# Extra weight sums of the down projection: the kept block copied from DRAM to DRAM, all sums in two bursts, and three fixed rooms for reading them back

## The chip, the cores and the metric

The kernel runs on one core of a Trainium2 chip. The metric is the device time of one execution in microseconds (us); the time of a kernel is the median of its runs. The core has a matrix engine (TensorE, in the profile PE, with its weight loads as PEld), a vector engine (VectorE, DVE), a scalar engine (ScalarE, ACT), a general engine (GpSimd, POOL) and a sync engine that here only issues DMAs (SyncE, SP). Sixteen DMA engines move data; SP's DMAs go through the queue that the profile calls q1, POOL's through q0, ACT's through q10. Engines run their instructions in order and wait for each other by semaphores.

## What is computed

One decoder layer on 256 tokens with 2048 features, all in float32. Two token mixers work in parallel on the same normalised input, a gated recurrence and a sliding-window attention with sinks; gates merge them; a squared-ReLU MLP of width 8192 follows. Cut to the lines that matter:

```python
h = rmsnorm(x, norm_mix_pre)
xr, yr, q, k, v, g_rnn, g_attn = split(h @ w_in)
y_rnn = rg_lru(conv(xr)) * gelu(yr)
y_att = attention(rope(q), rope(k), v, sinks)
mix = sigmoid(g_rnn) * (y_rnn @ w_rnn_proj) + sigmoid(g_attn) * (y_att @ w_attn_proj)
x = x + rmsnorm(mix @ w_out, norm_mix_post)
h = rmsnorm(x, norm_mlp_pre)
u = square(relu(h @ w_mlp_up))          # 2048 -> 8192
x = x + rmsnorm(u @ w_mlp_down, norm_mlp_post)   # 8192 -> 2048
```

## The kernel before

**Matrix products in three parts.** Every float32 operand is split in two, a high half in a format that PE takes at full rate and a low half that holds the rest. A product is three matmuls: high by high, high by low, low by high. The weights come through `Stream` (the object `ws`): chunks of 128 x 2048 are loaded in halves of 512 KB on SP (L87, into `wraw` or, late in the kernel, `xraw`), ACT rounds a half to `whi` (L109), DVE subtracts it to `wlo` (L110), PE multiplies. `load_to` and `split_to` run a few halves ahead of PE; `begin` is called at each step of the stream and steps the side jobs in `ws.side`.

**Order of the stages.** First `kx`: sixteen tiles that hold a piece of the key and value weights and of the transposed input, loaded on SP (L425) and used by the `kv` matmuls (L496). Then the gate weights and the input itself (`xq`, L433, for the norm's sums of squares, L502). Then four attention groups, each eight weight halves for a gate `g` and eight for `q`, with the rope of `q` on DVE (L592 to L596: `ra`, `rb`, `qr`) and PE's transposes of it (`pq`, L637) among the matmuls; then the recurrence, the merge of both mixers (gate by projection on DVE, L953 and L954, PE's transposes `ptr`, L936), the output projection, and the MLP in two halves, f = 0 and f = 1. Each half of the MLP has 16 up products of pairs (`up_pair`, `a_pair`) and two down passes (`down`, n = 0 and n = 1) over 16 weight chunks each.

**The down passes with fewer products.** For most down chunks PE forms seven block products in place of eight. This needs extra sums of the chunk's quarters (128 x 512 each): T1, T2, T3 and T4. A table (`KINDS`) says for each chunk how many of these are made ahead: all four (kind 4), two (kind 2) or none (kind 3); kind 1 is a plain chunk. There are 36 chunks of kinds 2 and 4, 18 in each half of the MLP.

**`sums_ahead(c)`** makes them for one chunk long before the down pass. It is a generator and each `yield` is one step of the weight stream. It loads the chunk (1 MB) on POOL into a room `early` (L370), waits four steps, lets DVE add T1 (L375), for kind 4 T3 (L377), and T2 (L378) in place, and stores T2 and the block next to it, the unchanged last quarter B21, to the DRAM tile `b` (L379, 512 KB, POOL). Two steps later it stores T3 and T1 (L383, 512 KB, kind 4), lets DVE add T4 into that last quarter (L385), and stores T4 (L386, 256 KB). L385 overwrites what the store of L379 reads, so DVE waits for that store at L385. `tc.issue_after(ws.latest_low.ins)` places each group of sums behind the latest weight half on DVE.

**`in_turn(n, every, wait)`** starts n of these generators, one each `every` steps after `wait` steps. It runs in five places: `in_turn(11, 4, 16)` in the attention groups, `in_turn(2, 6)` twice in the recurrence, `in_turn(8, 6, 1)` in the merge, `in_turn(6, 7, 4)` in the up products of f = 0 and `in_turn(7, 7)` in those of f = 1.

**Reading the sums back.** In the down pass the second half of a chunk is loaded from `b` (L80, SP) instead of from the weights, and the rest is read into a room `third` on POOL (L141, 768 KB, kind 4; L143, 256 KB, kind 2). `split` then rounds and subtracts these too (L159 `thi` on ACT, L160 `tlo` on DVE).

**Rooms.** `early`, `third`, the kept activations and the accumulators all share the pool `big`, twelve rooms of 1 MB under one tag (`unit`), given out in turn. A load into a room waits until the room's last reader is done. Before, each call of `ws.third` took a room of its own in this turn. In the second half of the down pass of f = 0, `between(p)` reads the normalised MLP input h2T back from DRAM into such rooms on SP.

**Order of the instructions.** A scheduler of the framework places the instructions of each engine by dependencies and priorities. An instruction without dependencies can be placed far ahead of where it stands in the code. DMAs on POOL's queue also wait for an earlier DMA of the same one of eight semaphores (`DMASW0` to `DMASW7` in the order below).

Of the kernel before, what the change touches and what calls it, by code (L numbers as in the profile page):

```python
# [18 lines left out]
F32 = mybir.dt.float32  # L19
# [3 lines left out]
ALU = mybir.AluOpType  # L23
# [186 lines left out]
def layer(tc, x, few, kx_first, kx_rest, pos_row, gains, w_q, w_xy, w_rg, w_g, w_rp, w_ap, w_out,  # L210
          w_up, w_dn, out):
    nc = tc.nc
# [11 lines left out]
    chunks = [None] * (FIRST // 2)  # L224
# [22 lines left out]
    sums, plain_down = {}, set()  # L247
# [7 lines left out]
    def unit(name, dt=F32R):  # L255
        return big.tile([P, 4, 2, S], dt, tag="U8", name=name)

    def flat(t):
        return t.rearrange("p a b c -> p (a b c)")

    ws = Stream(nc, wpool, chunks, sums)
# [104 lines left out]
    def sums_ahead(c):  # L366

        w = flat(unit("early", F32))
        t3, t1, t2, t4 = [w[:, quarter(i)] for i in range(4)]
        nc.gpsimd.dma_start(w, chunks[c])  # L370
        for i in range(4):
            yield
        v, four, (b, t) = nc.vector, sums[c] == "4", ws.summed[c]
        with tc.issue_after(ws.latest_low.ins):
            v.tensor_tensor(t1, t1, t3, ALU.add)  # L375
            if four:
                v.tensor_tensor(t3, t3, t2, ALU.add)  # L377
            v.tensor_tensor(t2, t2, t1, ALU.add)  # L378
        nc.gpsimd.dma_start(b, w[:, 1024:2048])  # L379
        for i in range(2):  # L380
            yield
        if four:
            nc.gpsimd.dma_start(t[:, 0:1024], w[:, 0:1024])  # L383
        with tc.issue_after(ws.latest_low.ins):
            v.tensor_tensor(t4, t4, t2, ALU.add)  # L385
        nc.gpsimd.dma_start(t[:, 1024:1536] if four else t, t4)  # L386
        yield

# [22 lines left out]
    def quarter(q):  # L411
        return slice(q * 512, q * 512 + 512)
# [6 lines left out]
    for k in range(KT):  # L419
        if k % 2 == 0:  # L420
            place, at = flat(unit(f"kx{k}", F32)), 0
        n = 512 + S + (KT if k == 0 else 0)
# [49 lines left out]
        return i  # L472

    ws.keep = behind_latest
    ws.third = lambda: flat(unit("third", F32))
    ws.kept = plain_down

    def part(k):
# [287 lines left out]
    def wide(t):  # L766
        return t.rearrange("p (f t) -> p f t", f=2)
# [212 lines left out]
    def u2(name):  # L980
        return pb.tile([P, 512], F32, tag="u2", bufs=4, name=name)
# [336 lines left out]
        ws.ahead(ws.at - 1)  # L1318

    for f in range(2):  # L1320
        uT = {}
        rooms = []
        if f:
            ws.side.append(in_turn(7, 7))
        full = []
        for p in range(PAIRS):
            u = u2("u")
            if f == 0 and p == 1:
                ws.side.append(in_turn(6, 7, 4))
            if f == 0 and p in (4, 6, 8):  # L1330
                nc.gpsimd.dma_start(h2T_away[p // 2 - 2], h2T[p // 2 - 1].bitcast(F32))
            if f == 0 and p < 2:
                up_pair(p, wide(u))
            else:
                a_pair(h2T, wide(u), PRIO if p == PAIRS - 1 else 0)
            full.append((p, u))
            if f == 0 and p == R2_AT:
                pump(99)
                spread_r2()
                ctx3.close()  # L1340
                pc = ctx2.enter_context(tc.tile_pool(name="pc", bufs=1))
                ws.more = lambda: pc.tile([P, 1024], F32, tag="xraw", name="xraw")
                ws.sums_room = lambda tag, n: pc.tile([P, n], F32R, tag=f"{tag}{n}", name=f"{tag}{n}")
            if f == 1 or p >= R2_AT:
                for q, u in full:
                    if q % 2 == 0:
                        rooms.append(unit(f"uT{f}{q}"))
                    room = rooms[-1][:, 2 * (q % 2) : 2 * (q % 2) + 2]
                    if q in SEVENS[f]:
                        three = pc.tile([P, 2, 3, P], F32R, tag="three", bufs=max(map(len, SEVENS)), name=f"three{f}{q}")  # L1350
                        uT[q] = three, flat(room).rearrange("p (a b c) -> p a b c", a=2, b=4)
                    else:
                        uT[q] = room
                    evacuate(f, q, u, uT[q])
                full.clear()
        order = [(1, 1), (1, 0), (0, 0), (0, 1)]
        if f == 0:
            for n in range(2):
                def finish(name, b, t, *part):
                    tb, i = name  # L1360
                    c = quarter(2 * n + i)
                    nc.vector.tensor_tensor(t, b, t, ALU.add)
                    nc.scalar.dma_start(acc_away[tb][:, c], t)

                def between(p):
                    if n and p in (4, 7, 10):
                        i = (p - 1) // 3
                        h2T[i] = unit(f"h2T{i}b")
                        nc.sync.dma_start(h2T[i].bitcast(F32), h2T_away[i - 1])

                down(f, n, uT, 2, order, finish, lambda ready: None, between)
            continue
        accs, x1 = [], []

        def acc(tb, q):
            return accs[q // 2][:, tb, quarter(q % 2)]

        def load_acc():
            accs.append(flat(unit("acc", F32)).rearrange("p (a b) -> p a b", a=2))
            for tb in range(TB):  # L1380
                nc.sync.dma_start(accs[-1][:, tb], acc_away[tb][:, n * 1024 : n * 1024 + 1024])

        def early(ready):
            for (tb, i), t in ready.items():
                nc.vector.tensor_tensor(t, t, acc(tb, 2 * n + i), ALU.add)

        def behind():
            for tb in range(TB):
                x1.append(flat(unit(f"x1{tb}", F32)))
                with tc.issue_after(ws.latest.ins):  # L1390
                    nc.sync.dma_start(x1[tb], x1_away[tb])

        def between(p):
            if p == 6:
                load_acc()
            if n == 0:
                return
            if p == 2:
                g3.append(flat(unit("g3", F32)))
            if 2 <= p < 6:  # L1400
                c = quarter(p - 2)
                nc.sync.dma_start(g3[0][:, c], gains[3][c].partition_broadcast(P))
            for k in {7: (0,), 8: (1, 2), 10: (3,)}.get(p, ()):
                tb, q = divmod(k, 2)
                nc.vector.tensor_tensor(acc(tb, q), acc(tb, q), g3[0][:, quarter(q)], ALU.mult)

        def finish(name, b, t, at, w, fold=lambda: None):
            tb, i = name
            q = 2 * n + i
            a = acc(tb, q)  # L1410
            if n == 0:
                nc.vector.tensor_tensor(a, b, t, ALU.add)
                nc.scalar.activation(t, a, AF.Square, accum_out=sq3[:, tb, q : q + 1])
                return
            p = slice(at, at + w)
            k = q + (at > 0)
            pin(nc.vector.tensor_tensor(a[:, p], b[:, 0:w], t[:, p], ALU.add))
            if not spare:
                spare.append(flat(unit("spare", F32)))
            pin(nc.scalar.activation(spare[0][:, p], a[:, p], AF.Square, accum_out=sq3[:, tb, k : k + 1]))  # L1420
            pin(nc.vector.tensor_tensor(t[:, p], a[:, p], g3[0][:, q * 512 + at : q * 512 + at + w], ALU.mult))
            last[tb, i] = t
            fold()
            if at + w < 512:
                return
            if i:
                r, to = [st[:, 12 + 2 * tb + k : 13 + 2 * tb + k] for k in range(2)]
                pin(nc.vector.tensor_reduce(r, sq3[:, tb, 0 : 4 + tb], AX.X, ALU.add))
                pin(nc.scalar.activation(to, r, AF.Sqrt, bias=eps, scale=1.0 / D))
                pin(nc.vector.reciprocal(r, to))  # L1430
                scaled[tb] = r
            for tb, qs in {(0, 1): ((0, (2, 0, 1, 3)),), (1, 1): ((1, (2, 0, 1, 3)),)}.get(name, ()):
                for k in qs:
                    c = quarter(k)
                    g = acc(tb, k) if k < 2 else last[tb, k - 2]
                    pin(nc.vector.scalar_tensor_tensor(x1[tb][:, c], g, scaled[tb], x1[tb][:, c], ALU.mult, ALU.add))
                    pin((nc.scalar if k % 2 else nc.sync).dma_start(o_v[tb][:, c], x1[tb][:, c]))

        n = 0
        g3, spare = [], []  # L1440
        down(f, n, uT, 2, order, finish, early, between)
        n = 1
        last, scaled = {}, {}
        down(f, n, uT, 2, [(0, 0), (0, 1), (1, 0), (1, 1)], finish, early, between, behind, True)
# [81 lines left out]
```

## Time and profile before

| | |
|---|---|
| median of 3 runs | 1518.93 us (1516.91 to 1519.06) |
| the profiled execution, its own time | 1525.07 us |
| its span | 1523.0 us |
| PE busy | 1487.0 us (98%) |
| DVE busy | 1174.3 us (77%) |
| ACT busy | 859.7 us (56%) |
| POOL busy | 92.6 us (6%) |
| moved by DMA | 403.20 MB, mean 265 GB/s |
| of this on POOL's queue q0 | 101.72 MB |

The profile is of one execution. A row of the groups gives line, engine, operation, output and inputs, shapes and count, then busy time and mean of one, then the engine's idle time just before and what ended most of it. In a timeline a row has start and duration, and in brackets the idle time before it with the releaser. In the waits a row reads "engine and line waited for engine and line: total, times, longest". A row of windows gives for a stretch its length, the busy time of each engine with the number of instructions, the mean granted TensorE clock (1.00 is full), the DMA engines' busy share and GB/s.

### The profile page before, as it was taken

The numbers are of one execution on the slowest core, as the hardware profiler recorded it, in microseconds if no ns is written. First come the engines' busy times: TensorE is split into PE (matmuls) and PEld (weight loads), VectorE is DVE, ScalarE is ACT, GpSimd is POOL, SyncE is SP. The second block draws the span as 40 slices with busy tenths as digits, with TensorE's granted clock in tenths as the row PEclk, the third lists the DMA queues.
The fourth block names the chain that finished last, engine by engine and source line by source line (L and its number), as shares of the span: only waits on it lengthen the run. The fifth ranks groups of instructions, "written<-read, shape, count | busy, mean of one in ns | idle before, by whom it ended". The sixth has DMA issues, their size and how long they took to land.

```text
span 1523.0 us, 20576 instructions
## 1 busy us (share of the span) xinstructions
PE 1487.0 (98%) x7536; PEld 1256.6 (83%) x7536; DVE 1174.3 (77%) x1543; ACT 859.7 (56%) x1213; POOL 92.6 (6%) x178
## 2 busy tenths in 40 slices
PE   9998999999999999989999899999999999999997
PEld 7886777888888888778889788888878888888876
DVE  6686777867869877566667788778978787779887
ACT  7662654646566666344445655566565555556663
POOL 0011110000000000010000010000000110000000
PEclk9999999999999999999999999999999999999998
DMA  9778876676756567888765888768898889679794
GB/s 350 242 248 307 295 258 207 206 254 214 258 188 221 181 220 255 304 313 274 275 215 196 309 304 307 264 226 296 291 346 271 308 295 330 222 257 324 244 343 172
DMA packets 106917, 403.20 MB, mean 265 GB/s; under 512 B 12224, under 2 KB 12480, under 8 KB 100672
## 3 DMA queue, kind: packets, MB, share of 16 engines
q1 hardware_dynamic: 82800, 294.93, 56.5%
q0 software_dynamic: 21136, 101.72, 18.1%
q10 hardware_dynamic: 2880, 5.24, 0.9%
q8 instruction: 59, 0.97, 0.3%
q14 instruction: 42, 0.34, 0.1%
HBM read 352.56 MB, written 49.28 MB: 264 GB/s over the span
## 4 chain that ended last, share of the span: by engine, by line
PE 74%; DMA 10%; issue 6%; DVE 6%; ACT 3%; POOL 1%; SPq 0%; DVEq 0%; POOLq 0%; ACTq 0%
PE ps L300 21%; PE ps L298 11%; PE s L1227 6%; PE dQ L1227 6%; DMA away<-early 3%; PE dP L1227 3%; PE pp L342 3%; PE pp L340 3%; PE pp L338 3%; DMA wraw<-away 3%; DVE wlo L110 2%; PE o L342 2%; PE o L340 2%; PE o L338 2%; PE dCs L1227 2%
## 5 line engine op out<-in xcount | busy, mean ns | idle before, releaser
L109 ACT CAST whi<-wraw 128x1024 fp32r<-128x1024 f32 x469 | 488.0, 1050 | 418.8 <-PE ps L300 82.2
L110 DVE TENSOR_TENSOR wlo<-wraw,whi 128x1024 fp32r<-128x1024 f32 x469 | 566.1, 1220 | 159.1 <-ACT whi L109 155.5
L300 PE MATMUL ps<-h2T,whi 128*128 128x512 f32 x576 | 143.5, 394 | 5.8 <-DVE st L450 5.8
L300 PEld LDWEIGHTS ps<-h2T,whi 128*128 128x128 f32 x576 | 107.3, 190 | 26.8 <-DVE u L1169 6.0
L300 PE MATMUL ps<-hT,whi 128*128 128x512 f32 x512 | 120.6, 391 | 0.0
L300 PEld LDWEIGHTS ps<-hT,whi 128*128 128x128 f32 x512 | 94.7, 188 | 19.5 <-issue 0.7
L338 PE MATMUL g<-whi,hT 128*128 128x512 f32 x256 | 103.0, 402 | 0.0
L340 PE MATMUL g<-wlo,hT 128*128 128x512 f32 x256 | 101.6, 397 | 1.3 <-DVE wlo L110 1.3
L342 PE MATMUL g<-whi,hT 128*128 128x512 f32 x256 | 101.3, 396 | 0.0
L159 ACT CAST thi<-third 128x1024 fp32r<-128x1024 f32 x88 | 69.7, 834 | 50.1 <-PE s L1227 37.3
L160 DVE TENSOR_TENSOR tlo<-third,thi 128x1024 fp32r<-128x1024 f32 x88 | 80.3, 953 | 14.5 <-ACT thi L159 14.5
L1227 PE MATMUL dQ<-whi,uT 128*128 128x512 f32 (+1 forms) x248 | 91.3, 387 | 0.0
L385 DVE TENSOR_TENSOR early<-early 128x512 f32<-128x512 f32 x36 | 24.9, 691 | 78.8 <-DMA away<-early 78.7
L298 PE MATMUL ps<-h2T,wlo 128*128 128x256 f32 x576 | 76.4, 283 | 0.0
L298 PEld LDWEIGHTS ps<-h2T,wlo 128*128 128x128 f32 x576 | 74.2, 191 | 2.3
L109 ACT CAST whi<-xraw 128x1024 fp32r<-128x1024 f32 x47 | 49.3, 1050 | 31.5 <-PE ps L300 12.4
L298 PEld LDWEIGHTS ps<-hT,wlo 128*128 128x128 f32 x512 | 63.7, 191 | 2.1 <-issue 0.8
L298 PE MATMUL ps<-hT,wlo 128*128 128x256 f32 x512 | 64.7, 283 | 0.0
L110 DVE TENSOR_TENSOR wlo<-xraw,whi 128x1024 fp32r<-128x1024 f32 x47 | 57.3, 1220 | 5.9 <-ACT whi L109 5.8
L1227 PE MATMUL s<-thi,uT 128*128 128x512 f32 x176 | 61.4, 390 | 0.0
L340 PEld LDWEIGHTS g<-wlo,hT 128*128 128x128 f32 x256 | 49.2, 192 | 11.5 <-DVE wlo L110 1.7
L338 PEld LDWEIGHTS g<-whi,hT 128*128 128x128 f32 x256 | 49.2, 192 | 10.9 <-issue 1.0
(322 smaller groups left out, 3059.2 us busy)
## 6 DMA issues: line engine op xcount, KB each, us to landing
wraw<-in_w_up SPq DMA_DIRECT2D x106, 512.0 KB, 5.1
early<-in_w_dn POOLq DMA_DIRECT2D x36, 1024.0 KB, 8.8
wraw<-in_w_dn SPq DMA_DIRECT2D x68, 512.0 KB, 5.6
wraw<-in_w_g SPq DMA_DIRECT2D x64, 512.0 KB, 5.0
wraw<-in_w_xy SPq DMA_DIRECT2D x64, 512.0 KB, 4.3
away<-early POOLq DMA_DIRECT2D x58, 512.0 KB, 5.6
third<-away POOLq DMA_DIRECT2D x22, 768.0 KB, 8.1
wraw<-in_w_q SPq DMA_DIRECT2D x32, 512.0 KB, 4.6
```

What stands on the lines that cost most here:

```text
L109: self.pin(self.nc.scalar.copy(hi, src))
L110: self.latest_low = self.pin(self.nc.vector.tensor_tensor(lo, src, hi.bitcast(F32), ALU.subtract))
L159: self.keep(self.nc.scalar.copy(hi, t))
L160: self.keep(v.tensor_tensor(lo, t, hi.bitcast(F32), ALU.subtract))
L298: mm(ps[:, f, 1, :], w, a[:, 0, :], start=False, stop=j == 1 and k == 7)
L300: mm(ps[:, f].rearrange("p a b -> p (a b)"), w, a.rearrange("p a b -> p (a b)"), start=kt == 0, stop=j == 3 and k == 7)
L338: mm(banks[tb][n], a[:, 0, t], hi[:, n * 512 : n * 512 + 512], start=first, stop=False)
L340: mm(banks[tb][n], a[:, 0, t], lo[:, n * 512 : n * 512 + 512], start=False, stop=False)
L342: mm(banks[tb][n], a[:, 1, t], hi[:, n * 512 : n * 512 + 512], start=False, stop=last)
L385: v.tensor_tensor(t4, t4, t2, ALU.add)
L1227: mm(b, a[x], w[y], start=not begun and i == 0, stop=tail and i == 2, skip_group_check=shared)
```

## The change

The unchanged quarter B21 is no longer stored from the room: a DMA on POOL copies it straight from the weights in DRAM to its place in the DRAM tile `b` (256 KB, one for each of the 36 chunks), written right behind the chunk's load. The sums come as two bursts one step apart, T1 and T3, then T2 and T4, and all stores follow one step after: T3 and T1 (kind 4), T2 (256 KB), T4. No sum overwrites what a store reads. `third` takes three rooms once and uses them in turn (the list is cleared at the start of each f, and in `behind` in f = 1). `in_turn` for the up products of f = 0 goes from (6, 7, 4) to (6, 6, 16), and h2T is read back one chunk earlier (p = 3, 6, 9 for 4, 7, 10).

```diff
         w = flat(unit("early", F32))
         t3, t1, t2, t4 = [w[:, quarter(i)] for i in range(4)]
+        v, four, (b, t) = nc.vector, sums[c] == "4", ws.summed[c]
         nc.gpsimd.dma_start(w, chunks[c])
+        nc.gpsimd.dma_start(b[:, 512:1024], chunks[c][:, 1536:2048])
         for i in range(4):
             yield
-        v, four, (b, t) = nc.vector, sums[c] == "4", ws.summed[c]
         with tc.issue_after(ws.latest_low.ins):
             v.tensor_tensor(t1, t1, t3, ALU.add)
             if four:
                 v.tensor_tensor(t3, t3, t2, ALU.add)
+        yield
+        with tc.issue_after(ws.latest_low.ins):
             v.tensor_tensor(t2, t2, t1, ALU.add)
-        nc.gpsimd.dma_start(b, w[:, 1024:2048])
-        for i in range(2):
-            yield
+            v.tensor_tensor(t4, t4, t2, ALU.add)
+        yield
         if four:
             nc.gpsimd.dma_start(t[:, 0:1024], w[:, 0:1024])
-        with tc.issue_after(ws.latest_low.ins):
-            v.tensor_tensor(t4, t4, t2, ALU.add)
+        nc.gpsimd.dma_start(b[:, 0:512], t2)
         nc.gpsimd.dma_start(t[:, 1024:1536] if four else t, t4)
         yield
...
-    ws.third = lambda: flat(unit("third", F32))
+    third_rooms = []
+
+    def third():
+        if len(third_rooms) < 3:
+            third_rooms.append(flat(unit("third", F32)))
+        else:
+            third_rooms.append(third_rooms.pop(0))
+        return third_rooms[-1]
+
+    ws.third = third
...
     for f in range(2):
+        third_rooms.clear()
...
-                ws.side.append(in_turn(6, 7, 4))
+                ws.side.append(in_turn(6, 6, 16))
...
-                    if n and p in (4, 7, 10):
-                        i = (p - 1) // 3
+                    if n and p in (3, 6, 9):
+                        i = p // 3
...
         def behind():
+            third_rooms.clear()
```

In the changed kernel the load is L371, the copy L372, the sums L376, L378, L381 and L382, the stores L385 to L387; the rope is L602 to L606, and what comes behind the first lines of the attention stands 10 to 12 lines lower.

## Prediction

> **What bounds the kernel now.** I read the page first, then what TensorE (PE) waited for, then the timelines around those waits, the granted clock there, and last the first 50 us. The page:
>
> ```profile
> span 1523.0 us, 20576 instructions
> PE 1487.0 (98%) x7536; PEld 1256.6 (83%) x7536; DVE 1174.3 (77%) x1543; ACT 859.7 (56%) x1213; POOL 92.6 (6%) x178
> L385 DVE TENSOR_TENSOR early<-early 128x512 f32<-128x512 f32 x36 | 24.9, 691 | 78.8 <-DMA away<-early 78.7
> ```
>
> PE is busy for 98% of the span, so the change can gain only what PE loses, and costs whatever newly starves PE. VectorE (DVE) idles 78.8 us ahead of L385, the last sum, which overwrites what the store of L379 is still reading. What reaches PE is in its waits (total us, times, longest):
>
> ```profile
> PE pq L637 <- DVE qr L596: 9.7, 4, 3.5
> PE ptr L936 <- DVE g L954: 5.6, 2, 3.8
> PE s L1227 <- DVE tlo L160: 4.2, 4, 2.0
> ```
>
> The timelines tie the first two to L385 (start, duration, idle before). DVE in the rope of attention group 1, then PE there, then DVE and PE in the merge:
>
> ```profile
> 137.18 0.68 DVE L593 TENSOR_TENSOR rb<-q,ss 128x512 f32<-128x512 f32 x1
> 140.93 0.69 DVE L385 TENSOR_TENSOR early<-early 128x512 f32<-128x512 f32 x1 [3.07 <-DMA away<-early]
> 141.88 0.42 DVE L596 TENSOR_TENSOR qr<-ra,rb 128x256 f32<-128x256 f32 x1
> 136.81 0.63 PE L637 MATMUL pq<-ident,qr 128*128 128x128 f32 x4 [3.50 <-DVE qr L596]
> 142.44 1.09 PE L637 MATMUL pq<-ident,qr 128*128 128x128 f32 x4 [2.70 <-DVE qr L596]
> ...
> 664.33 0.69 DVE L385 TENSOR_TENSOR early<-early 128x512 f32<-128x512 f32 x1 [6.29 <-DMA away<-early]
> 667.27 1.29 DVE L954 TENSOR_TENSOR g<-g,m 128x512 f32<-128x512 f32 x2
> 668.11 1.09 PE L936 MATMUL ptr<-ident,g 128*128 128x128 f32 x4 [3.83 <-DVE g L954]
> ```
>
> The rope is half done at 137.18, L385 then blocks DVE for 3.07 us, and the transposes wait 2.70. At 664 a 6.29 us block becomes a 3.83 us wait. After these stops PE also runs at a lower granted clock (window, its length, PE busy; the figure ahead of the DMA share is PEclk):
>
> ```profile
> 130.00:145.00 15.00, 8.80 (x37) 6.84 (x36) 11.93 (x18) 4.32 (x5) 1.61 (x3) 0.90 0.72 245
> 192.00:208.00 16.00, 12.48 (x59) 9.48 (x59) 8.90 (x14) 4.57 (x6) 2.68 (x5) 0.79 0.76 263
> 658.00:674.00 16.00, 12.17 (x50) 9.86 (x49) 9.64 (x14) 5.83 (x6) 1.62 (x3) 0.89 0.80 293
> 610.00:625.00 15.00, 13.19 (x61) 10.66 (x60) 11.39 (x14) 6.59 (x7) 1.45 (x3) 1.00 0.73 242
> ```
>
> Idle time plus length times missing clock: 6.20 + 1.50, 3.52 + 3.36, 3.83 + 1.76, 1.81 + 0. Together 22.0 us: the most that removing the block on DVE is worth here.
>
> **The sums.** All of a chunk's sums (0.69 us each, same count as before) come in two bursts, with the stores behind. DVE's order at the same rope, before (ra, rb, qr: the rope; wlo: low halves of the weights):
>
> ```order
> L593 TENSOR_TENSOR rb_1797<-q0_1551,ss_233 128x512
> L110 TENSOR_TENSOR wlo62_1803<-wraw62_1716,whi62_1802 128x1024 [waits DMAHW7_49,Activation_49]
> L595 TENSOR_TENSOR qr_1795<-ra_1796,rb_1797 128x8x32 [waits DVE_49]
> L596 TENSOR_TENSOR qr_1795<-ra_1796,rb_1797 128x8x32
> L592 TENSOR_TENSOR ra_1827<-q1_1552,cc_232 128x512
> L593 TENSOR_TENSOR rb_1828<-q1_1552,ss_233 128x512
> L385 TENSOR_TENSOR early_1680<-early_1680 128x512 [waits DMASW4_49]
> ```
>
> and now:
>
> ```order
> L603 TENSOR_TENSOR rb_1804<-q0_1557,ss_233 128x512
> L381 TENSOR_TENSOR early_1685<-early_1685 128x512 [waits DVE_49]
> L605 TENSOR_TENSOR qr_1802<-ra_1803,rb_1804 128x8x32 [waits DVE_49]
> L606 TENSOR_TENSOR qr_1802<-ra_1803,rb_1804 128x8x32
> L382 TENSOR_TENSOR early_1685<-early_1685 128x512 [waits DVE_49]
> L110 TENSOR_TENSOR wlo62_1812<-wraw62_1724,whi62_1811 128x1024 [waits DMAHW7_49,Activation_49]
> L602 TENSOR_TENSOR ra_1836<-q1_1558,cc_232 128x512
> L603 TENSOR_TENSOR rb_1837<-q1_1558,ss_233 128x512
> ```
>
> The wait on a software-DMA semaphore (DMASW) at L385 is gone; the last sums wait only for DVE's own results. So I credit all 22.0 us. Bounds: the sums still stand between the rope's steps, so one stop of the 3.50 us kind with its clock loss, about 5 us, may stay; against that, DVE is freer elsewhere by the rest of its 78.8 us of idle time.
>
> **The copies.** Each of 36 chunks gets a 256 KB copy from DRAM to DRAM on POOL's queue. POOL's order at the start, before (early: a 1 MB load; away: a sum's block in DRAM):
>
> ```order
> L577 AFFINE_SELECT mask1_462<-mask1_462 128x256 [waits Pool_49]
> L370 DMA early_827<-in_w_dn 128x2048 [waits DMAHW2_49,DMAHW3_49,DVE_49,Activation_49]
> L379 DMA away1024169_69<-early_827 128x1024 [waits DMASW0_49,DVE_49]
> L370 DMA early_973<-in_w_dn 128x2048 [waits DMAHW7_49,DMAHW0_49,Activation_49]
> L370 DMA early_1081<-in_w_dn 128x2048 [waits DMAHW4_49,DMAHW3_49,Activation_49]
> ```
>
> and now, where 24 rows like the second and third stand between the third and the fourth:
>
> ```order
> L372 DMA away1024169_69<-in_w_dn 128x512
> L587 AFFINE_SELECT mask1_462<-mask1_462 128x256 [waits Pool_49]
> L372 DMA away1024170_71<-in_w_dn 128x512
> L372 DMA away1024243_119<-in_w_dn 128x512 [waits DMASW1_49]
> L371 DMA early_827<-in_w_dn 128x2048 [waits DMAHW2_49,DMASW2_49,DMAHW3_49,DVE_49,Activation_49]
> L372 DMA away1024260_139<-in_w_dn 128x512 [waits DMASW4_49]
> L371 DMA early_972<-in_w_dn 128x2048 [waits DMAHW0_49,DMASW5_49,DMAHW7_49,DVE_49,Activation_49]
> L371 DMA early_1081<-in_w_dn 128x2048 [waits DMAHW3_49,DMASW6_49,DMAHW4_49,DVE_49,Activation_49]
> ```
>
> A copy reads an input and writes a fresh tile, so it waits for nothing but an earlier copy of its lane. All 36 stand at the very start, with ten between early_827 and early_972 of which the last is shown. The second and third 1 MB loads no longer stand behind a store that waits for DVE. Before, they left here (POOL: start, duration, idle before):
>
> ```profile
> 10.68 0.67 POOL L370 DMA_DIRECT2D early<-in_w_dn  x1 [8.34 <-ACT whi L489]
> 86.82 0.54 POOL L379 DMA_DIRECT2D away<-early  x1 [75.47 <-DVE early L378]
> 87.37 1.07 POOL L370 DMA_DIRECT2D early<-in_w_dn  x2
> ```
>
> So 36 x 256 KB = 9.44 MB and 2.10 MB move into the first 40 us. What is there already (windows as above; the last two figures are the DMA share and GB/s), and SP's issues:
>
> ```profile
> 10.00:20.00 10.00, 10.00 (x45) 8.26 (x45) 8.84 (x22) 7.33 (x15) 0.67 (x1) 1.00 1.03 411
> 20.00:30.00 10.00, 10.00 (x45) 8.28 (x45) 9.12 (x21) 7.46 (x14) 0.00 (x0) 1.00 1.03 398
> 30.00:40.00 10.00, 8.73 (x38) 6.86 (x37) 3.73 (x13) 9.95 (x22) 0.00 (x0) 1.00 0.77 290
> ...
> 4.05 8.35 SPq L425 DMA_DIRECT2D kx<-in_kx_rest  x10
> 13.06 5.12 SPq L87 DMA_DIRECT2D wraw<-in_w_g  x4
> 19.47 9.33 SPq L433 DMA_DIRECT2D xq<-in_x  x8
> 29.21 8.02 SPq L87 DMA_DIRECT2D wraw<-in_w_g  x4
> ```
>
> From 10 to 30 us the DMA engines are full, at 411 GB/s. Is there slack behind the loads? ACT, DVE and PE at that point:
>
> ```profile
> 29.15 0.64 ACT L502 ACTIVATE xq<-xq 128x512 f32<-128x512 f32 x1 [0.85 <-DMA xq<-in_x]
> 35.62 1.22 DVE L110 TENSOR_TENSOR wlo<-wraw,whi 128x1024 fp32r<-128x1024 f32 x1
> 36.90 0.50 PE L340 MATMUL g<-wlo,hT 128*128 128x512 f32 x1 [1.27 <-DVE wlo L110]
> ```
>
> None: ACT waits for xq, DVE's weight half waits behind work on it, and PE waits 1.27 us for that half. What delays xq delays PE by as much, and PE at 98% never makes it up.
>
> How much of the extra traffic goes ahead of xq is set by how the two queues share. Between 16 and 18 us, with a 1 MB load in flight on q0, and between 142 and 146 us, with a 256 KB store:
>
> ```profile
> q0 software_dynamic: 77, 0.62, 75.0%
> q1 hardware_dynamic: 74, 0.21, 26.0%
> ...
> q1 hardware_dynamic: 126, 0.50, 36.9%
> q0 software_dynamic: 80, 0.26, 17.3%
> ```
>
> 77 packets against 74: turns go by packet, and q0's bigger packets (8 KB) get three quarters. The Trainium skill ("DMA: Bandwidth & Descriptors", section on issuing engines that are not separate DMA queues) says that DMAs from all issuing engines interleave on the same 16 DMA engines. It speaks against an extra stream at a full spot, and the two queues' shares here bear it out.
>
> The store's 80 packets hold 0.26 MB, some 4 KB each if the 16 smallest only signal. At 4 KB a copy is four packets on each of 16 engines: 144 for all copies, 8 for early_827 at 8 KB, 16 for the two pulled loads, 168 in all. q1 needs more turns than that before xq is in: 16 kx of 384 KB at 3 KB packets are 128, four halves of 512 KB at 4 KB are 32, and eight xq of 256 KB at 2 to 4 KB are 32 to 64, thus at least 192 (packet sizes of kx and xq are an estimate from the rows of their tensors). So everything goes ahead: (9.44 + 2.10) MB / 411 GB/s = 28.1 us. The trace of before holds no DRAM-to-DRAM transfer. I price it by bytes once, like the 256 KB store above, whose 0.26 MB took 17.3% of 4 us, 0.69 us. The bounds: twice that, if reading and writing each take a turn (+23.0 us), and below it, if its packets are smaller (next part). The same page of the Trainium skill, in its Specifications, puts a core's share of DRAM bandwidth at about 358 GB/s; by that, an estimate, 11.54 MB would take 32.2 us and the sum be 4.1 us higher. The 411 GB/s of loads alone go past it, so the measurement decides.
>
> Add 2 us for a lowered clock after PE's stop, between the 1.50 and 3.36 above.
>
> **Third rooms, pacing, reloads.** Taking three rooms once removes no transfer; the third loads now follow each other's rooms. They feed tlo, whose waits cost PE 4.2 us in all, so the effect lies between -4.2 and about +4. I take -1, since the sums no longer hold DVE. Pacing 6 for 7 and the reloads one chunk earlier move DMAs only where PE does not wait for them: 0, at most +-2.
>
> **Sum.** +28.1 + 2 - 22.0 - 1 = +7.1 us. The profiled execution took 1525.07 us, 2.07 more than its span and 6.1 above the median of 1518.93. On its own time the sum gives 1532.2, on the median 1526.0, which I predict. A measurement here can tell about 0.2%, 3 us.
>
> **The rivals.**
>
> Copies in smaller packets (other side, faster). If each 2 KB row of a copy is a packet, eight per engine and copy, q0 yields two thirds to q1: in q1's 192 to 216 turns some 26 copies (208 packets, 6.8 MB) pass before xq, and the rest later, when the DMA share is 0.77. Shift 6.8 / 0.411 = 16.5 us, so 16.5 + 2 - 22.0 - 1 = -4.5: 1514.4. The point at which it turns is a shift of 21 us. For it: the slice is 2 KB wide in DRAM. Against: the 256 KB stores also have 2 KB rows, and go at about 4 KB.
>
> Copies cost double by byte: +7.1 + 23.0 = +30, half of that +18.6: 1537 to 1549. For it: each copy reads and writes HBM. Against: loads and stores both cost their bytes once.
>
> DVE is blocked anyway, by loads delayed in the same queue or by sums in the rope: the 22.0 stay, +29, about 1548. Against: the rows above; the loads come four weight steps ahead.
>
> Burst and gain cancel within 3 us: part of the burst falls where q1 is not yet full (the first 10 us), 1519.
>
> **How the numbers follow.** Burst in full and stalls gone, 1522 to 1531: 0.42. Smaller packets, 1509 to 1516: 0.28. Cancelling: 0.15. Copies dearer: 0.10. DVE still blocked: 0.05. Faster by over 0.2%: 0.28 and a little of the down passes' lower bound, 0.30. Same: 0.15. Slower: 0.55. The range leaves out the tail of the two last rivals and the deepest gain: 1511 to 1543; the likeliest case's own is 1522 to 1531.
>
> **What would show it.** In the profile after: 36 copies issued on POOL from about 2 us; the DMA share near 1.0 until some 62 us; xq's first cast on ACT at about 57 us instead of 29.15; PE stops in the kv steps; then no idle time ahead of the last sum and no pq or ptr wait over 1 us, and granted clock 1.00 at those spots. Wrong if xq arrives less than 20 us late, if a copy takes more than its 256 KB of DMA time, or if pq still waits.

## The result, and the profile after

The changed kernel took 1529.43 us (median of 4 runs, 1528.78 to 1531.1) against 1518.99 us beside it: 10.4 us longer, ratio 1.0071 with a 95% interval of 1.0054 to 1.0089. The forecast was 1526.0. Its profiled execution took 1531.1 us, only 6.0 above that of before, because the profiled execution of before lay 6.1 above its median and this one 1.7. The page after:

```profile
span 1529.3 us, 20618 instructions
PE 1490.0 (97%) x7536; PEld 1255.3 (82%) x7536; DVE 1177.9 (77%) x1543; ACT 861.4 (56%) x1213; POOL 112.1 (7%) x214
```

What PE waited for (total us, times, longest):

```profile
PE g L340 <- DVE wlo L110: 12.2, 2, 11.4
PE kv L506 <- ACT hT L490: 8.8, 7, 2.3
PE ps L300 <- DVE st L451: 5.5, 1, 5.5
PE g L338 <- ACT whi L109: 2.4, 2, 1.8
PE s L1237 <- DVE tlo L160: 1.2, 2, 0.6
```

The waits for the rope (`pq`, 9.7 us before) and the merge (`ptr`, 5.6) are gone from the list, and so is DVE's wait at the last sum. New are 8.8 us in the kv steps, and the wait for a weight half has grown from 1.3 to 12.2 us; both lie in the first 70 us.

The start: POOL's first and last copies and its loads, SP's issues, and the engines behind xq, in the same form as before:

```profile
1.83 0.69 POOL L372 DMA_DIRECT2D away<-in_w_dn  x1
2.88 3.19 POOL L372 DMA_DIRECT2D away<-in_w_dn  x6
35.95 0.58 POOL L371 DMA_DIRECT2D early<-in_w_dn  x1 [0.65 <-DVE ang L536]
51.01 0.52 POOL L372 DMA_DIRECT2D away<-in_w_dn  x1 [0.93 <-DMA xq<-in_x]
52.22 0.55 POOL L371 DMA_DIRECT2D early<-in_w_dn  x1 [0.68 <-DMA xq<-in_x]
53.34 0.54 POOL L371 DMA_DIRECT2D early<-in_w_dn  x1 [0.57 <-DMA away<-in_w_dn]
...
35.49 17.71 SPq L434 DMA_DIRECT2D xq<-in_x  x8
54.72 15.62 SPq L87 DMA_DIRECT2D wraw<-in_w_g  x4
...
54.66 0.63 ACT L512 ACTIVATE xq<-xq 128x512 f32<-128x512 f32 x1 [2.98 <-DMA xq<-in_x]
65.72 0.63 ACT L512 ACTIVATE xq<-xq 128x512 f32<-128x512 f32 x1 [2.48 <-DMA xq<-in_x]
70.00 0.79 PE L340 MATMUL g<-wlo,hT 128*128 128x512 f32 x1 [11.42 <-DVE wlo L110]
```

The copies leave from 1.83 us on, at most seven in flight, until 51. The two pulled loads follow. ACT's first work on xq moves from 29.15 to 54.66 us and its last from xq waits until 65.72, and the matmul that waited 1.27 us at 36.90 now waits 11.42 and starts at 70.00: 33.1 us later. The windows of these stretches (PE busy first, then clock, DMA share, GB/s at the end):

```profile
10.00:20.00 10.00, 6.35 (x18) 4.18 (x18) 3.26 (x6) 3.39 (x7) 3.86 (x9) 0.83 1.03 353
20.00:30.00 10.00, 7.71 (x22) 5.43 (x23) 4.42 (x9) 4.00 (x9) 3.74 (x8) 0.66 1.00 396
30.00:40.00 10.00, 8.17 (x27) 5.27 (x26) 5.76 (x16) 4.24 (x9) 4.00 (x8) 0.83 1.03 391
40.00:50.00 10.00, 7.09 (x24) 3.97 (x23) 4.64 (x10) 3.83 (x6) 3.06 (x6) 0.94 1.02 410
50.00:60.00 10.00, 8.00 (x30) 5.94 (x28) 1.90 (x3) 4.03 (x8) 1.71 (x4) 0.89 1.01 386
60.00:70.00 10.00, 0.00 (x0) 0.00 (x1) 1.82 (x7) 5.10 (x16) 0.00 (x0) 0.62 0.69 277
70.00:80.00 10.00, 10.00 (x31) 7.98 (x32) 8.74 (x25) 8.06 (x11) 0.00 (x0) 0.70 0.71 231
...
160.00:176.00 16.00, 16.00 (x89) 13.12 (x89) 12.75 (x19) 7.38 (x8) 2.71 (x5) 1.00 0.97 361
214.00:230.00 16.00, 16.00 (x94) 13.18 (x94) 13.60 (x19) 6.76 (x8) 2.71 (x5) 1.00 0.90 316
672.00:688.00 16.00, 16.00 (x74) 13.25 (x73) 12.32 (x15) 6.83 (x7) 2.54 (x5) 1.00 0.90 300
```

The DMA engines are full until past 60 us. Behind the stop the granted clock is 0.70 for ten microseconds, which is 3 us. The last three rows are the ropes of groups 1 and 2 and the second stop of the merge: PE is busy throughout, at full clock, where it lost 7.7, 6.9 and 5.6 us before. DVE in the rope of group 1 no longer stops:

```profile
165.38 0.68 DVE L603 TENSOR_TENSOR rb<-q,ss 128x512 f32<-128x512 f32 x1
165.99 0.68 DVE L381 TENSOR_TENSOR early<-early 128x512 f32<-128x512 f32 x1
166.92 0.42 DVE L606 TENSOR_TENSOR qr<-ra,rb 128x256 f32<-128x256 f32 x1
167.26 0.68 DVE L382 TENSOR_TENSOR early<-early 128x512 f32<-128x512 f32 x1
169.60 0.68 DVE L603 TENSOR_TENSOR rb<-q,ss 128x512 f32<-128x512 f32 x1
171.66 0.41 DVE L606 TENSOR_TENSOR qr<-ra,rb 128x256 f32<-128x256 f32 x1
```

How late PE stands can be followed by taking the same matmul in both timelines. The table gives the start before, and how much later (+) or earlier (-) it starts in the changed kernel and in some of the runs below.

| matmul | before, us | after | burst | half | late | best | held2 |
|---|---|---|---|---|---|---|---|
| first q of group 0 | 51.24 | +36.0 | +28.2 | +14.6 | +5.5 | 0.0 | +0.2 |
| scores, group 0 | 85.94 | +35.5 | +27.7 | +14.8 | +5.2 | -0.2 | +0.1 |
| scores, group 1 | 147.13 | +27.5 | +26.2 | +14.9 | -2.8 | -2.8 | -7.9 |
| scores, group 2 | 206.94 | +20.9 | +25.0 | +12.8 | -9.4 | -9.4 | -14.5 |
| first of the last merge stage, `pp` | 590.39 | +20.8 | +25.0 | +12.6 | -9.6 | -9.3 | -14.7 |
| first output projection | 731.22 | +13.3 | +24.1 | +14.1 | -17.1 | -16.8 | -20.4 |
| first down product, f = 0 | 1009.59 | +12.8 | +23.9 | +14.7 | -17.0 | -15.8 | -20.4 |
| first up product, f = 1 | 1173.52 | +9.7 | +21.8 | +12.4 | -19.5 | -18.3 | -22.2 |
| near the end | 1512.73 | +6.3 | +21.9 | +10.3 | -24.7 | -22.9 | -27.4 |

Reading the "after" column: +35.5 at the start, then -8.0 and -6.7 in the two ropes, -7.5 in the merge, and -6.5 in the down passes (-3.1 and -3.4).

### The profile page after: what moved, and what is told of

Same layout as the page of the kernel before. It is cut to its first block, busy times and chain, and to the rows that moved or that the text cites. A ratio compares the mean times of both kernels' runs of the same rounds, so it can differ in the third digit from the quotient of the medians.

```text
span 1529.3 us, 20618 instructions
## 1 busy us (share of the span) xinstructions
PE 1490.0 (97%) x7536; PEld 1255.3 (82%) x7536; DVE 1177.9 (77%) x1543; ACT 861.4 (56%) x1213; POOL 112.1 (7%) x214
## 3 DMA queue, kind: packets, MB, share of 16 engines
q10 hardware_dynamic: 2880, 5.24, 0.9%
## 4 chain that ended last, share of the span: by engine, by line
PE 88%; DMA 6%; DVE 3%; ACT 1%; issue 1%; SPq 0%; DVEq 0%; ACTq 0%
PE ps L300 21%; PE ps L298 11%; PE s L1237 6%; PE dQ L1237 6%; PE pp L340 4%; PE pp L342 4%; PE pp L338 4%; PE g L340 4%; PE g L338 4%; PE g L342 4%; PE dP L1237 3%; PE q L338 2%; PE q L342 2%; PE q L340 2%; PE o L342 2%; PE o L340 2%
## 5 line engine op out<-in xcount | busy, mean ns | idle before, releaser
L340 PE MATMUL g<-wlo,hT 128*128 128x512 f32 x256 | 101.9, 398 | 12.2 <-DVE wlo L110 12.2
L300 PEld LDWEIGHTS ps<-hT,whi 128*128 128x128 f32 x512 | 94.7, 188 | 19.5 <-issue 0.7
L340 PEld LDWEIGHTS g<-wlo,hT 128*128 128x128 f32 x256 | 49.2, 192 | 22.6 <-DVE wlo L110 12.8
L338 PEld LDWEIGHTS g<-whi,hT 128*128 128x128 f32 x256 | 49.1, 192 | 14.1 <-ACT whi L109 3.2
L342 PEld LDWEIGHTS g<-whi,hT 128*128 128x128 f32 x256 | 49.2, 192 | 10.5
```

The source lines that it names most:

```text
L300: mm(ps[:, f].rearrange("p a b -> p (a b)"), w, a.rearrange("p a b -> p (a b)"), start=kt == 0, stop=j == 3 and k == 7)
L338: mm(banks[tb][n], a[:, 0, t], hi[:, n * 512 : n * 512 + 512], start=first, stop=False)
L340: mm(banks[tb][n], a[:, 0, t], lo[:, n * 512 : n * 512 + 512], start=False, stop=False)
L342: mm(banks[tb][n], a[:, 1, t], hi[:, n * 512 : n * 512 + 512], start=False, stop=last)
```

## The experiments

Medians of before in the three groups of runs were 1515.34, 1518.45 and 1516.31 us; its single runs spread from 1512.7 to 1523.6. The kernels whose sums do not stop DVE spread by 6 us at most, mostly by 1 to 4, so absolute times are compared among them.

**burst: the copies alone.** Before, with the copies to tiles that nothing reads.

```diff
         nc.gpsimd.dma_start(w, chunks[c])
+        nc.gpsimd.dma_start(spot[c], chunks[c][:, 1536:2048])
```

> The kernel before, with 36 copies of 256 KB from DRAM to DRAM added right behind the loads of the chunks, into tiles that nothing reads (extra work); sums, stores and waits as before, and the second and third 1 MB loads stay behind their store. Theory A, the copies alone make the stop at the start: in the changed kernel 11.54 MB of extra traffic shifted PE by 35.5 us, so 9.44 MB shift it by about 30, and with the stops on DVE kept the time is 1519 + 30 = 1549 us (1545 to 1553). At the 411 GB/s of loads, bytes once, it would be +25, 1544. Rival B, the start is late because of the two pulled loads or the new order of the sums: the copies alone cost under 10 us, below 1529.

1546.56 us, +31.2 on the medians; ratio 1.02 (1.0169 to 1.0231). The stops on DVE are still there, and PE's matmul of 36.90 starts at 63.81:

```profile
DVE early L388 <- DMA away<-early: 74.7, 29, 6.0
...
63.81 0.80 PE L340 MATMUL g<-wlo,hT 128*128 128x512 f32 x1 [7.17 <-DVE wlo L110]
```

The burst makes the loss, and 9.44 MB shift PE by 26.9 us, not by the 23.0 of their bytes at 411 GB/s. With the lowered clock behind the stop it is 28.2 at the first q; the +31.2 rests on a median of before that lies some 3 us below that of two other groups.

**half: 18 of the copies.**

```diff
+        if c in first_half:
+            nc.gpsimd.dma_start(spot[c], chunks[c][:, 1536:2048])
```

> The same with the first 18 of the 36 copies only (extra work that nothing reads). Theory A, each copy costs its bytes on engines that are full from 10 to 34 us, plus a lowered clock of 2 to 3 us once: half of the bytes, 13.5 + 2.5 = +16, 1535 us (1531 to 1538). Rival, a threshold: what fits into the less busy first 10 us is free, so that the first half costs little and the second nearly all: below +8, 1527.

1531.34 us, +16.0; ratio 1.01 (1.0063 to 1.0136). The same matmul starts at 51.48, +14.6. So no threshold: the first 18 copies cost 14.6 us and the other 18 cost 12.3.

**nocopy: no copy at all.** SP reads B21 from the weights when the chunk is wanted.

```diff
-        nc.gpsimd.dma_start(b[:, 512:1024], chunks[c][:, 1536:2048])
...
             if summed:
-                self.latest = self.nc.sync.dma_start(t, summed[0])
+                self.nc.sync.dma_start(t[:, 0:512], summed[0][:, 0:512])
+                self.latest = self.nc.sync.dma_start(t[:, 512:1024], chunk[:, 1536:2048])
```

> The changed kernel without any copy: SP reads the kept block B21 straight from the weights when the chunk is wanted, in a DMA of its own (256 KB beside the 256 KB of T2), so no byte more moves than before. Theory A, the gain on DVE is independent of the burst: -22 for the ropes and the merge, -3 for the down passes, +5 and some clock for the two 1 MB loads that still go to the start: -18, 1501 us (1496 to 1505). Rival, the stops went away only because the burst shifted the stages against each other, or SP's 36 more DMAs cost PE: 1510 or more.

1501.61 us; ratio 0.9911 (0.9878 to 0.9943). The gain stands without the burst.

**late: each copy behind its chunk's store.**

```diff
+        done = nc.gpsimd.dma_start(b[:, 0:512], t2)
         nc.gpsimd.dma_start(t[:, 1024:1536] if four else t, t4)
+        with tc.issue_after(done.ins):
+            nc.gpsimd.dma_start(b[:, 512:1024], chunks[c][:, 1536:2048])
```

> The changed kernel with each copy queued on POOL behind the store of its chunk's T2, so that the copies lie spread over the kernel. Theory A, only the place of the copies costs: as without copies, 1501 us (1496 to 1506), since the DMA engines are some 70 percent busy there. Rival, the copies cost wherever they are, by contention with the weights or by delaying POOL's later loads: 1508 or more.

1500.83 us; ratio 0.9901 (0.9866 to 0.9936). The same copies, spread, cost nothing that can be measured. At the start only the two pulled loads are left:

```profile
42.36 0.50 PE L340 MATMUL g<-wlo,hT 128*128 128x512 f32 x1 [1.40 <-DVE wlo L110]
```

That is 5.5 us late for 2.10 MB; 5.1 by bytes.

**mid: all copies in one burst at 229 us,** behind the eleventh chunk's store.

```diff
+        if c == burst_at:
+            with tc.issue_after(done.ins):
+                for k in ws.summed:
+                    nc.gpsimd.dma_start(ws.summed[k][0][:, 512:1024], chunks[k][:, 1536:2048])
```

> The kernel with the late copies, but all 36 copies in one burst at the end of the attention groups, behind the store of the eleventh chunk, at about 229 us, where POOL has nothing to do for 51 us and the weights ask for some 250 and then 124 to 156 GB/s with halves loaded ahead. Theory A, a burst costs PE only where the DMA engines are full and nothing is loaded ahead: 1500 to 1504 us, against 1500.8 with the copies spread. Rival, 9.44 MB in a burst cost their DMA time wherever they stand: +23 to +27, 1524 to 1528 us.

1501.47 us; ratio 0.9898 (0.987 to 0.9926), as late. The DMA engines are full there too, but PE does not stop (PE busy 15.00 of 15):

```profile
225.00:240.00 15.00, 15.00 (x67) 10.67 (x66) 9.45 (x17) 6.17 (x9) 6.89 (x13) 1.00 1.00 347
240.00:255.00 15.00, 15.00 (x101) 12.95 (x100) 13.14 (x33) 7.57 (x10) 5.79 (x11) 1.00 1.00 352
255.00:270.00 15.00, 14.97 (x89) 12.75 (x89) 15.00 (x31) 9.56 (x31) 7.33 (x14) 1.00 0.97 343
```

In late, without the burst, these windows move 306, 172 and 124 GB/s at a DMA share of 0.80, 0.53 and 0.39: the loads leave room. So it is not the burst as such: it costs where the loads that PE waits for already fill the DMA engines. This run also speaks against contention as a cost of its own.

**best: the two loads held back too.** The loads of the second and third chunk wait in POOL's order behind the first chunk's store. The edit ties every later load, too, behind a store made before it.

```diff
+        if c in held:
+            for i in range(3):
+                yield
...
-        nc.gpsimd.dma_start(w, chunks[c])
+        with tc.issue_after(stored[0].ins) if stored else ExitStack():
+            nc.gpsimd.dma_start(w, chunks[c])
```

> The kernel with the late copies, and the second and third 1 MB load queued on POOL behind the first chunk's store of T2, three steps later, as they stood before the change. Theory A, these 2.10 MB at the start cost their bytes: PE stood 5.2 us later behind the start with them (2.10 MB at 411 GB/s are 5.1 us), so the time goes from 1500.8 to 1495.6 us (1494 to 1498). Rival, the 5.2 us come from something else at the start, such as the order of the rest: 1500 to 1502.

1501.35 us: no better than late, so the number failed. The table shows why: 5.4 us are saved at the start, but only 2.6 in the first rope in place of 8.0. POOL's loads, ACT and PE there:

```profile
95.81 1.60 POOL L377 DMA_DIRECT2D early<-in_w_dn  x3
111.07 1.05 ACT L109 CAST whi<-wraw 128x1024 fp32r<-128x1024 f32 x1 [2.75 <-DMA wraw<-in_w_q]
114.33 1.04 ACT L109 CAST whi<-wraw 128x1024 fp32r<-128x1024 f32 x1 [2.21 <-DMA wraw<-in_w_g]
115.92 1.22 PE L731 MATMUL pt<-ident,s 128*128 128x128 f32 x8 [3.42 <-ACT pT L733]
```

Three 1 MB loads leave together, since a third one had slipped in behind the same store. ACT waits for weight halves, its copies for the attention stand behind those casts, and PE waits 3.42 us for them. This is the fault of the change in small.

**held2: the fourth load held two steps longer.** The lines are against those of best.

```diff
-    stored, held = [], to_sum[1:3]
+    stored, held = [], dict(zip(to_sum[1:4], (3, 3, 2)))
```

> Late copies, the second and third load held behind the first chunk's store as in the run named best, and the fourth load held two steps longer, so that it goes behind the second chunk's store and only two 1 MB loads leave together at about 95 us in place of three. Theory A, in the run named best three loads at once held back the weight halves (10 to 12 us to land in place of 4), ACT and PE's transposes waited 3.4 us for them, and the lowered clock added 2; without that the saving at the start shows: 1496 us (1494 to 1498). Rival, the saving at the start is lost elsewhere again: 1500 to 1502.

1496.86 us (1496.32 to 1497.8); ratio 0.987 (0.9843 to 0.9898). Two loads leave together, and the wait for `pt` on ACT's `pT` is gone:

```profile
96.05 1.08 POOL L377 DMA_DIRECT2D early<-in_w_dn  x2
...
PE ps L300 <- DVE st L459: 5.8, 1, 5.8
PE ptr L954 <- DVE g L972: 1.6, 1, 1.6
PE g L340 <- DVE wlo L110: 1.3, 1, 1.3
```

**nocopy2: the same holding without copies.** The edits of nocopy and held2 together.

> The same holding of the loads in the kernel without copies, where SP reads B21 from the weights. Theory A: 1496 us (1494 to 1499), as with the late copies. Rival, SP's extra DMAs cost: 1500 or more.

1496.59 us (1494.68 to 1497.96); ratio 0.9864 (0.983 to 0.9898). This and held2 beat both kernels, by some 20 us the one before and 33 us the changed one, and cannot be told apart.

**rest: only the other edits.** Before, with the three rooms, the pacing and the reloads of the change.

> The kernel before with only the other edits: three rooms for the thirds used in turn, the loads of the up products of f = 0 paced at (6, 6, 16), h2T read back one chunk earlier; sums and stores as before. Theory A (the prediction's term): -1 us, within 3 us of the kernel before. Rival, the 6.5 us that the profiled execution of the changed kernel gained in the down passes come from these edits: -5 to -7 us.

1515.31 us against 1518.45; ratio 0.9983 (0.9967 to 0.9998): -3.1 us on the medians, -0.3 to -5 by the interval. Between the theories.

**norest: the changed kernel without the other edits.**

> The changed kernel with those other edits undone: copies at the start, sums in two bursts, but rooms, pacing and reloads as before. Theory A: +1 us against the changed kernel, 1530 us (1528 to 1533). Rival, the edits bring the gain in the down passes: 1534 to 1537.

1531.01 us (1530.95 to 1533.44), 1.6 above the changed kernel.

**bestnorest: best without the other edits.**

> Late copies, held loads, sums in two bursts, and the other edits undone: the sums' change alone without any burst at the start. Theory A: the ropes and the merge give -22 us against the kernel before by themselves, 1496 to 1498 us, and the other edits are worth about 1 us beside it. Rival, they are worth 5 to 7 us here: 1501 to 1503.

1501.36 us against 1501.35: nothing. The absolute time expected for theory A was missed with that of best, and lies in the rival's range, for the same reason: PE has the same stop, 3.1 us ahead of `pt`. The comparison with best holds: the sums' change gives the gain by itself.

## Why the prediction was right

**The sign and the cause held.** All 36 copies went to the start, ahead of xq, as POOL's order said, and burst shows that they alone make most of the loss. The total was closer than its largest term: the burst with its clock came out at 36.0 us in place of 30.1, the total only 3.4 us above the forecast. Small gains beyond the forecast made up the rest (below), and that is partly luck.

**The gain on DVE, -22.0 forecast.** PE gained 8.0 + 6.7 in the ropes and 7.5 in the merge, 22.2 us. Idle time plus missing clock, window by window, was the right price, and no stop of the 3.50 us kind stayed in the rope.

**The burst, +28.1 forecast, was mis-sized.** PE's matmul came 33.1 us late. The two pulled loads are 5.5 us of this (late), close to the 5.1 of their bytes; the copies are 26.9 (burst) where 23.0 stood, 17% more, and 0.7 us comes only with both. The copies' packets are of the size assumed. The page after counts on q0

```profile
q0 software_dynamic: 21712, 101.72, 18.0%
```

packets, MB and share; before there were 21136 packets. The stores given up (36 x 128), those added (36 x 64) and 36 copies of 64 packets of 4 KB with 16 signals each come to just this: -4608 + 2304 + 2880 = 576.

The bytes that went ahead were right, too. Up to the start of that matmul (36.90 us before, 70.00 after) all queues had moved

```profile
DMA packets 4752, 13.25 MB, mean 359 GB/s; under 512 B 526, under 2 KB 654, under 8 KB 4621
DMA packets 7917, 24.77 MB, mean 354 GB/s; under 512 B 1135, under 2 KB 1263, under 8 KB 7530
```

That is 11.52 MB more, where the sum had 11.54. What the price by bytes missed is the rate: 11.52 MB in 33.1 us are 348 GB/s, and the sum took the 411 GB/s of the loads' best ten microseconds for the whole stretch. Between 10 and 20 us the copies and loads together made 353 GB/s at a DMA share of 1.03, and from 10 to 60 us the mean is 387. By an estimate from this, 50 us x (1 - 387/411), about 3 of the 5 us lie there; the rest is not assigned. Between 10 and 20 us a 4 KB packet of the copies took 0.16 us at the median and up to 2.1; why was not settled.

So one sign that the prediction had named for being wrong did appear: a copy takes more than its 256 KB of DMA time, 0.75 us against 0.64. The rows behind the price had one direction at a time, and the upper bound of the double was far too high.

The Trainium skill's limit for a core's share of DRAM ("DMA: Bandwidth & Descriptors", Specifications, about 358 GB/s) gave an estimate nearer to the result, 32.2 us for the burst where 33.1 were measured, but not by its reason. From 10 to 35 us, with only copies on q0, the queues moved (packets, MB, share)

```profile
q0 software_dynamic: 1553, 5.10, 57.6%
q1 hardware_dynamic: 1642, 4.19, 43.9%
```

all of it read from DRAM, and the 5.10 MB of copies written there as well: (9.29 + 5.10) MB / 25 us = 576 GB/s. The measurement goes past the limit again. The first row also gives the price of a copy a second time: 57.6% of 25 us for 5.10 MB is 0.74 us for 256 KB.

**The lowered clock, +2 forecast,** was 2.9: +33.1 at the matmul, +36.0 at the first q.

**The other edits, -1 forecast:** -3.1 in rest, -1.6 between norest and the changed kernel, 0 in bestnorest. The -6.5 us that the two profiles show in the down passes are more than this. In rest's profile they are -8.0, but in norest's, which lacks these edits, they are -6.0 as well, so most of them is not due to the edits. The runs of before differ by 10 us among themselves, and the profiled one is on the slow side. With 0 to -3 us for these edits, the changed kernel's sum is 35.5 - 22.2 = 13.3, less 0 to 3: +10.3 to +13.3. Measured is +10.4.

**The rivals.** Smaller packets: fallen, by the count of packets and by the 33.1 us. Copies at double price: fallen, 17% in place of 100%. DVE blocked anyway: fallen, no wait left. Cancelling through a free first 10 us: fallen, half shows the first copies as the dearer ones. Of what was to show it, the first cast on xq was expected at 57 us and came at 54.66; but each later xq stood behind more of q0's packets, and the last wait for one ended at 65.72.

## What to carry to other kernels

A DMA that depends on nothing can be placed far from where it is written, here at the very start, and 36 small ones become one large burst: look at the order on the issuing engine, and tie such a DMA to something that it should follow. Price a burst by what it delays: at a point where loads fill the DMA engines and nothing is held ready, every byte costs (burst, half), and at another, where the loads leave room (mid), the same bytes are free. A holding edge can make the next burst: three loads released at once lost much of what the holding had saved (best), two did not (held2).

## What the runs showed of the hardware

A copy of 256 KB from DRAM to DRAM among full queues cost 0.75 us (burst, 26.9 us / 36), against 0.64 us by its bytes at 411 GB/s. Copies and loads together ran at 353 to 410 GB/s in the windows from 10 to 60 us of the changed kernel. In the same kernel DRAM took 576 GB/s of reads and writes from one core's queues over 25 us.
